# Gate products of an RG-LRU layer on Trainium2: two channel tiles in one group of 64-row matmuls, and a dummy square root ahead of the first x^T transfer

## The chip, the cores and the metric

The kernel runs on one core of one Trainium2 chip. A core has five engines, each with its own in-order instruction queue: TensorE (PE, with its weight loads shown apart as PEld), VectorE (DVE), ScalarE (ACT), GpSimd (POOL) and SyncE (SP, which here only issues transfers). They meet through semaphores. 16 DMA engines move data between the chip's memory (HBM) and the core's SBUF; TensorE writes into PSUM, which has eight banks of 128 x 512 float32. The metric is the device time of one execution in microseconds (us), as the median of several runs.

## The reference, cut to what matters

One layer: an FFN, then a mixer with two branches, then a second FFN, at sequence length 512 and model width 1024, in float32. The change touches the recurrent branch, on 1024 channels that form 16 blocks of 64:

```python
xr = causal_conv(xr, conv_w[l], conv_b[l])                    # 4 taps
xb = xf.reshape(b, s, LRU_BLOCKS, LRU_BLOCK)                  # 16 blocks of 64 channels
r  = sigmoid(einsum('bshi,hij->bshj', xb, wa) + ba)           # one 64x64 matrix per block
ig = sigmoid(einsum('bshi,hij->bshj', xb, wx) + bx)
log_a = -LRU_C * r * softplus(-lam)
a = exp(log_a)
u = sqrt(-expm1(2.0 * log_a)) * (ig * xf)
h[t] = a[t] * h[t-1] + u[t]                                   # scan over the sequence
y_a = (hr * gelu(xg)) @ w_lru_out[l]
```

At the very start, the first FFN multiplies the normalised input by `ffn1_w1` and `ffn1_w3`; the kernel works on x transposed (x^T), tile by tile of 128 channels.

## The kernel before, in words

**Precision.** Every float32 operand of a matmul is split into a high part (rounded, written by ScalarE) and a low part (the rest, written by VectorE), and each product is three matmuls: high by high, low by high, high by low. The function `split2` (from L189) does this for activations, `split_to` (from L149) for weights: L156 on ScalarE, L157 on VectorE.

**Units.** A projection of 128 output channels is a "unit": `unit` takes the next weight tile (`get`, which also splits the weights two units ahead and loads raw ones further ahead), takes a PSUM bank and runs 24 matmuls of 128 x 512 (`mm_feat`, L201 to L203). After every 12 of them it calls `point()`.

**The plan.** `later(n, fn, rank)` puts a piece of work n points ahead; `point()` counts one and runs what is due, by rank and then by the order in which it was put there. That sets where in each engine's queue the piece stands. There is no other scheduler: each engine then works through its queue in order.

**The stage of the change.** After the first FFN come units xr 0 to 7 (the recurrent input; xr 0 to 3 inside the function before), wg 0 to 7 (gates of the merge), wk 0 and 1, four products for v, wq 0 and 1, xg 0 to 7. Point 9 is the middle of unit wg0, point 13 that of wg2, point 17 that of wg4, point 21 that of wg6, point 25 that of wk0. Put among them by the tables at the file's end, for channel tile i (128 channels, two blocks of 64):

- `conv(i)` at `CONV_AT[i]`: L814 on ScalarE and three L816 on VectorE.
- `rg_gates(i)` at `RG_AT[i]` = 7, 11, 13, 15, 17, 19, 21, 23: splits the tile (L191 on ScalarE, L192 on VectorE, into `xcs`); two points later (`RG_LAG`) `products`: two banks, r and i, and six matmuls (L832) in three pairs. One of a pair uses rows 0 to 63 of the array, the other rows 64 to 127, each with a 64 x 128 weight that holds a block's two matrices side by side; one point later `gates`: four tanh of 64 x 512 on ScalarE (L837, L840), which empty the two banks, and L841 on VectorE.
- `rg_decay(i)` at `DECAY_AT[i]`: L852 and L853 on ScalarE, and one point later L856 to L858 on VectorE.
- `rg_scan(i)` at `SCAN_AT[i]`: a Sqrt on ScalarE (L866), later L869 and the scan L870 on VectorE.
- one point after each wg unit `gate_out` (L894 on ScalarE), which empties the unit's bank; after each wk unit `k_out` (L905 to L911), after each v product `v_out`, after each wq unit `q_out` (L943, L945), after each xg unit `y_out`, which needs the scan's result.

PSUM banks are handed out in turn, eight in all, so the ninth request waits until the first of the eight was read.

**The start.** Nine warm-up matmuls on zeros (L603); x^T tile 0 is loaded by a transfer that ScalarE issues (L591), then a Sqrt of a tiny tile (L609) loads the table that holds Sqrt; the other first transfers are issued by SP (`vec`, then the first weights and x^T tiles). Then, for each of eight x^T tiles, ScalarE writes the high part (L643), VectorE the low part (L644), and nine matmuls follow (L650 to L652). A hardware transfer signals one of eight semaphores in turn, so the ninth waits for the first.

Of the kernel before, what the change touches and what calls it, by code (L numbers as in the profile page):

```python
# [12 lines left out]
AF = mybir.ActivationFunctionType  # L13
ALU = mybir.AluOpType

P = 128
# [15 lines left out]
V_CW, V_CB, V_BA, V_BX, V_LAM, V_BG, V_G1, V_SINK, V_N = 0, 32, 40, 48, 56, 64, 80, 88, 104  # L32
# [19 lines left out]
def hybrid_layer(ctx: ExitStack, tc: tile.TileContext, a: dict, out: bass.AP):  # L52
    nc = tc.nc
    act, dve, pool, pe, sp = nc.scalar, nc.vector, nc.gpsimd, nc.tensor, nc.sync
# [8 lines left out]
    def slot(shape, dt=F32, name="s"):  # L63
        uid[0] += 1
        return sb.tile(shape, dt, tag="slot", name=f"{name}_{uid[0]}")

    def bank(name="ps"):
        uid[0] += 1
        return pp.tile([P, 512], F32, tag="ps", name=f"{name}_{uid[0]}")
# [14 lines left out]
    bxh = cp.tile([P, 2, KT], F32, name="bxh")  # L84
# [76 lines left out]
    def get(nm, i, ahead=2, rawahead=3):  # L161

        k = st["get"]
        assert order[k] == (nm, i), (order[k], nm, i)
        dma_to(k + 1 + ahead)
        split_to(k + 1 + ahead)
        dma_to(st["split"] + rawahead)
        st["get"] += 1
        return pairs.pop(k)
# [5 lines left out]
    def later(n, fn, rank=1):  # L175
        uid[0] += 1
        due.append((now[0] + n, rank, uid[0], fn))
# [11 lines left out]
    def split2(hi, lo, src):  # L189

        act.activation(hi, src, AF.Copy)  # L191
        dve.tensor_tensor(out=lo, in0=src, in1=f32(hi), op=ALU.subtract)  # L192
# [14 lines left out]
    def unit(nm, i, **kw):  # L207
        w = get(nm, i)
        ps = bank("f")
        mm_feat(ps, w, **kw)  # L210
        return ps
# [12 lines left out]
    def rstd_of(ssq, scale=1.0, during=lambda q: None):  # L224

        n = ssq.shape[-1]
        w = 1 if n == 2 else n
        v, q, r, e, r2 = (small(w, x) for x in ("v", "q", "r", "e", "r2"))
        if n == 2:
            dve.tensor_scalar(out=v, in0=ssq[:, 0:1], scalar1=ssq[:, 1:2], scalar2=D * EPS, op0=ALU.add, op1=ALU.add)  # L230
        else:
            dve.tensor_scalar(out=v, in0=ssq, scalar1=D * EPS, scalar2=None, op0=ALU.add)
        act.activation(q, v, AF.Sqrt)
        during(q)
        dve.reciprocal(r, q)
        if w == 1:
            dve.scalar_tensor_tensor(out=e, in0=r, scalar=v, in1=r, op0=ALU.mult, op1=ALU.mult)
        else:
            dve.tensor_tensor(out=e, in0=r, in1=r, op=ALU.mult)
            dve.tensor_tensor(out=e, in0=e, in1=v, op=ALU.mult)  # L240
        s = scale * D**0.5
        dve.tensor_scalar(out=e, in0=e, scalar1=-0.5 * s, scalar2=1.5 * s, op0=ALU.mult, op1=ALU.add)
        dve.tensor_tensor(out=r2, in0=r, in1=e, op=ALU.mult)
        return r2
# [345 lines left out]
    def load_x(k, q=sp):  # L590
        q.dma_start(out=xts[k // 2][:, k % 2, :], in_=a["xT"][k * P : (k + 1) * P, :])  # L591
# [10 lines left out]
    for _ in range(WARM):  # L602
        pe.matmul(psw, warm[:, :P], warm, start=True, stop=True)  # L603

    load_x(0, act)

    tiny = small(4, "tiny")
    dve.memset(tiny, 1.0)
    act.activation(tiny, tiny, AF.Sqrt)  # L609
    sp.dma_start(out=vec, in_=a["vec"])  # L610
    for kp in range(KT // 2):
        load_w(0, kp)
# [18 lines left out]
    ps = [bank("f") for _ in range(NS)]  # L631
# [28 lines left out]
    r = rstd_of(s4, during=lambda q: act.activation(tiny, q, AF.Silu))  # L660
# [129 lines left out]
    def rg_load():  # L790
        r = slot([P, KT, P], name="rgraw")
        for nm, cs in (("rg_a_w", (0, 64)), ("rg_x_w", (64, 0))):
            v = a[nm].rearrange("(i two) p q -> two p i q", two=2)
            for par, c in enumerate(cs):
                pool.dma_start(out=r[64 * par : 64 * par + 64, :, c : c + 64], in_=v[par])
        hi = slot([P, KT, P], F32R, name="rghi")
        lo = slot([P, KT, P], F32R, name="rglo")
        act.activation(hi, r, AF.Copy)
        dve.tensor_tensor(out=lo, in0=r, in1=f32(hi), op=ALU.subtract)
        return hi, lo  # L800

    rgw = rg_load()
# [4 lines left out]
    def hcol(base, i):  # L807
        return bhalf[:, base - V_BA + i : base - V_BA + i + 1]
# [11 lines left out]
    def rg_gates(i):  # L820
        s0 = lru[i]
        s1 = slot([P, 2, SEQ], name="ig_e")
        lru[i] = (s0, s1)
        xs = slot([P, 2, SEQ], F32R, name="xcs")
        xc, t, ig = s0[:, 0, :], s0[:, 1, :], s1[:, 0, :]
        split2(xs[:, 0, :], xs[:, 1, :], xc)

        def products():
            ps = bank("r"), bank("i")
            for n, (w, x) in enumerate(((0, 0), (1, 0), (0, 1))):  # L830
                for p_, r_ in zip(ps, (slice(0, 64), slice(64, P))):
                    pe.matmul(p_, rgw[w][r_, i, :], xs[r_, x, :], start=n == 0, stop=n == 2)  # L832

            def gates():
                lo_, up = slice(0, 64), slice(64, P)
                for p_, r_ in zip(ps, (lo_, up)):
                    act.activation(t[r_], p_[r_], AF.Tanh, scale=0.5, bias=hcol(V_BA, i)[r_])  # L837

                for par, (p_, r_, o_) in enumerate(((ps[0], up, lo_), (ps[1], lo_, up))):
                    act.activation(ig[o_], p_[r_], AF.Tanh, scale=0.5, bias=bxh[r_, par, i : i + 1])  # L840
                dve.scalar_tensor_tensor(out=ig, in0=ig, scalar=1.0, in1=xc, op0=ALU.add, op1=ALU.mult)  # L841

            later(1, gates, 2)

        later(RG_LAG, products)

    def rg_decay(i):
        s0, s1 = lru[i]  # L850
        t, ig, e = s0[:, 1, :], s1[:, 0, :], s1[:, 1, :]
        act.activation(e, t, AF.Exp, scale=cneg[:, i : i + 1], bias=cneg[:, i : i + 1])  # L852
        act.activation(t, t, AF.Tanh, scale=chalf[:, i : i + 1], bias=chalf[:, i : i + 1])  # L853

        def factors():
            dve.scalar_tensor_tensor(out=ig, in0=e, scalar=1.0, in1=ig, op0=ALU.add, op1=ALU.mult)  # L856
            dve.scalar_tensor_tensor(out=e, in0=e, scalar=1.0, in1=t, op0=ALU.add, op1=ALU.mult)
            dve.tensor_scalar(out=e, in0=e, scalar1=-1.0, scalar2=1.0, op0=ALU.mult, op1=ALU.add)  # L858

        later(1, factors, 3)  # L860

    def rg_scan(i):
        s0, s1 = lru[i]
        t, ig, a_ = s0[:, 1, :], s1[:, 0, :], s1[:, 1, :]

        act.activation(t, t, AF.Sqrt, scale=0.25)  # L866

        def scan():
            dve.tensor_tensor(out=ig, in0=t, in1=ig, op=ALU.mult)  # L869
            dve.tensor_tensor_scan(t, a_, ig, 0.0, op0=ALU.mult, op1=ALU.add)  # L870
            lru[i] = s0

        later(SCAN_LAG[i], scan, 3)
# [6 lines left out]
    for i, p in enumerate(RG_AT):  # L880
        later(p, lambda i=i: rg_gates(i))
    for i in range(8):
        later(DECAY_AT[i], lambda i=i: rg_decay(i), 3)
        later(SCAN_AT[i], lambda i=i: rg_scan(i), 3)
# [11 lines left out]
    for i in range(8):  # L896
        ps = unit("wg", i)
# [16 lines left out]
    for i in range(2):  # L914
        ps = unit("wk", i)
# [8 lines left out]
    for t in range(NT):  # L924
        ps = bank("v")
# [22 lines left out]
    for i in range(2):  # L948
        ps = unit("wq", i)
# [12 lines left out]
    for i in range(8):  # L962
        ps = unit("xg", i)
# [121 lines left out]
    for nm, i in att_units:  # L1085
        if nm == "lru":
            w = get(nm, i) if i else w_lru
            ps = bank("f")
# [5 lines left out]
        ps = unit(nm, i)  # L1094
# [4 lines left out]
    w = get("wao", 0)  # L1099
# [14 lines left out]
    for i in range(8):  # L1114
        if i:
            w = get("wao", i)
        ps = bank("f")
# [33 lines left out]
ATT_STEP = 2.2  # L1151
ATT_LAG = (1, 1, 4, 1, 3, 1)
RG_LAG = 2
DECAY_AT = (11, 15, 17, 19, 21, 23, 25, 27)
SCAN_AT = (29, 29, 30, 30, 31, 31, 32, 32)
SCAN_LAG = (1, 2, 2, 3, 3, 4, 4, 5)
NSLOT = 42
# [59 lines left out]
```

## Time and profile before

| | us |
|---|---|
| median of 3 runs (1138.6 to 1138.85) | 1138.76 |
| profiled execution | 1138.66 |
| its span | 1136.9 |
| TensorE busy | 1128.2 |
| VectorE busy | 778.7 |
| ScalarE busy | 582.2 |

The granted TensorE clock was 0.998 over the span. The profile lists, for one execution, how long each engine was busy, the span in 40 equal slices (each digit the busy share in tenths), the chain of work that ended last, followed back from the end, groups of equal instructions, waits with what ended them, and instructions in order of time. A row of the last view has the start in us from the span's start, the duration, the engine, the line of the kernel, the operation, the output and the inputs by the program's names, the shape and a count; in square brackets stands the idle time of the engine just before and what ended it. Matmuls overlap in the array: what counts there is the distance from start to start, not the duration.

### The profile page before, as it was taken

How to read it: one execution, taken by the hardware profiler on the slowest of the kernel's cores; microseconds unless marked ns; L12 is line 12 of the kernel's file. 1: busy time of each engine (PE TensorE's matmuls, PEld its weight loads, DVE VectorE, ACT ScalarE, POOL GpSimd, SP SyncE). 2: the span in 40 equal slices, each digit the busy share in tenths (PEclk: the TensorE clock that was granted, in tenths of full speed). 3: DMA queues.
4: the chain of work that ended last, by engine and by line, in shares of the span. 5: the costliest groups of instructions: out<-in, count | busy, mean ns of one | idle time of the engine just before them, and what ended most of it. 6: DMA issues, size and time to landing. Idle time of an engine off the chain costs nothing.

```text
span 1136.9 us, 17091 instructions
## 1 busy us (share of the span) xinstructions
PE 1128.2 (99%) x6691; PEld 1001.0 (88%) x6691; DVE 778.7 (68%) x1183; ACT 582.2 (51%) x1036; POOL 340.7 (30%) x257
## 2 busy tenths in 40 slices
PE   9999999999999999999999999999999999999997
PEld 7889999988889977888888888889899999998886
DVE  5997889885436745684778854667968678985313
ACT  7445555564325369944656652356445555574211
POOL 0148677500001000001555640000655567700000
PEclk9999999999999999999999999999999999999999
DMA  9943223264314311334122333532123332254101
GB/s 343 158 132 112 96 92 111 82 216 157 104 55 146 132 56 56 90 96 130 56 85 83 93 109 98 176 118 93 39 93 112 112 103 84 93 193 176 40 19 55
DMA packets 36800, 124.93 MB, mean 110 GB/s; under 512 B 4400, under 2 KB 5936, under 8 KB 36720
## 3 DMA queue, kind: packets, MB, share of 16 engines
q1 hardware_dynamic: 34128, 115.15, 30.3%
q0 software_dynamic: 2448, 8.43, 3.8%
q8 instruction: 52, 0.85, 0.3%
q10 hardware_dynamic: 144, 0.26, 0.1%
q14 instruction: 28, 0.23, 0.1%
HBM read 116.50 MB, written 7.33 MB: 109 GB/s over the span
## 4 chain that ended last, share of the span: by engine, by line
PE 97%; DVE 2%; ACT 0%; issue 0%; DVEq 0%
PE f L201 11%; PE f L202 11%; PE f L203 11%; PE c L454 10%; PE c L453 10%; PE c L452 10%; PE acc L220 8%; PE acc L221 8%; PE acc L219 8%; PE pt L1032 1%; PE s L996 1%; PE s L995 1%; PE tr L292 1%; PE r L832 1%; PE o L1048 1%; PE o L1049 1%
## 5 line engine op out<-in xcount | busy, mean ns | idle before, releaser
L201 PE MATMUL f<-uT,whi 128*128 128x512 f32 (+1 forms) x536 | 197.1, 368 | 0.0
L202 PE MATMUL f<-uT,wlo 128*128 128x512 f32 (+1 forms) x536 | 195.3, 364 | 0.3 <-DVE wlo L157 0.3
L203 PE MATMUL f<-uT,whi 128*128 128x512 f32 (+1 forms) x536 | 195.0, 364 | 0.0
L219 PE MATMUL acc<-whi,hT 128*128 128x512 f32 x352 | 137.1, 390 | 0.0
L220 PE MATMUL acc<-wlo,hT 128*128 128x512 f32 x352 | 137.0, 389 | 0.0
L221 PE MATMUL acc<-whi,hT 128*128 128x512 f32 x352 | 136.9, 389 | 0.0
L201 PEld LDWEIGHTS f<-uT,whi 128*128 128x128 f32 x536 | 101.1, 189 | 18.4 <-issue 2.9
L192 DVE TENSOR_TENSOR wlo<-S,whi 128x1024 fp32r<-128x1024 f32 x68 | 112.9, 1660 | 4.0 <-ACT whi L191 3.7
L453 PE MATMUL c<-Xh,wlo 128*128 128x256 f32 x408 | 115.5, 283 | 0.0
L454 PE MATMUL c<-Xl,whi 128*128 128x256 f32 x408 | 115.5, 283 | 0.0
L453 PE MATMUL c<-uT,wlo 128*128 128x256 f32 x408 | 115.5, 283 | 0.0
L454 PE MATMUL c<-uT,whi 128*128 128x256 f32 x408 | 115.5, 283 | 0.0
L452 PE MATMUL c<-Xh,whi 128*128 128x256 f32 x408 | 115.5, 283 | 0.0
L452 PE MATMUL c<-uT,whi 128*128 128x256 f32 x408 | 115.5, 283 | 0.0
L202 PEld LDWEIGHTS f<-uT,wlo 128*128 128x128 f32 x536 | 101.2, 189 | 16.1 <-DVE wlo L157 0.7
L203 PEld LDWEIGHTS f<-uT,whi 128*128 128x128 f32 x536 | 101.1, 189 | 16.1
L1016 POOL TENSOR_SCALAR P<-P,d 128x256 f32<-128x256 f32 (+1 forms) x64 | 63.8, 1011 | 55.5 <-DVE d L1014 33.2
L452 PEld LDWEIGHTS c<-Xh,whi 128*128 128x128 f32 x408 | 78.3, 192 | 0.0
L452 PEld LDWEIGHTS c<-uT,whi 128*128 128x128 f32 x408 | 78.3, 192 | 0.0
L453 PEld LDWEIGHTS c<-uT,wlo 128*128 128x128 f32 x408 | 78.3, 192 | 0.0
L453 PEld LDWEIGHTS c<-Xh,wlo 128*128 128x128 f32 x408 | 78.3, 192 | 0.0
L454 PEld LDWEIGHTS c<-Xl,whi 128*128 128x128 f32 x408 | 78.3, 192 | 0.0
(309 smaller groups left out, 2684.5 us busy)
## 6 DMA issues: line engine op xcount, KB each, us to landing
raw_w2a<-in_w2a_dram SPq DMA_DIRECT2D x22, 512.0 KB, 3.7
raw_w1b<-in_w1b_dram SPq DMA_DIRECT2D x22, 512.0 KB, 4.0
raw_w3b<-in_w3b_dram SPq DMA_DIRECT2D x22, 512.0 KB, 3.9
raw_w2b<-in_w2b_dram SPq DMA_DIRECT2D x22, 512.0 KB, 4.2
raw_w3a<-in_w3a_dram SPq DMA_DIRECT2D x21, 512.0 KB, 4.4
raw_w1a<-in_w1a_dram SPq DMA_DIRECT2D x20, 512.0 KB, 4.4
raw_wg<-in_wg_dram SPq DMA_DIRECT2D x16, 512.0 KB, 3.8
raw_xr<-in_xr_dram SPq DMA_DIRECT2D x8, 512.0 KB, 4.1
```

Of the source, the lines that this page charges most:

```text
L192: dve.tensor_tensor(out=lo, in0=src, in1=f32(hi), op=ALU.subtract)
L201: pe.matmul(ps[:, c0:c1], wh[:, s], h_, start=k == 0, stop=False)
L202: pe.matmul(ps[:, c0:c1], wl[:, s], h_, start=False, stop=False)
L203: pe.matmul(ps[:, c0:c1], wh[:, s], l_, start=False, stop=k == KT - 1)
L219: pe.matmul(acc[n], x[:, 0, c], wh[:, s], start=first, stop=False)
L220: pe.matmul(acc[n], x[:, 0, c], wl[:, s], start=False, stop=False)
L221: pe.matmul(acc[n], x[:, 1, c], wh[:, s], start=False, stop=last)
L292: pe.transpose(ps[:, k * P : (k + 1) * P], hg[:, kk * P : (kk + 1) * P], ident)
L452: pe.matmul(ps, wh[:, s], xh, start=first, stop=False, skip_group_check=True)
L453: pe.matmul(ps, wl[:, s], xh, start=False, stop=False, skip_group_check=True)
L454: pe.matmul(ps, wh[:, s], xl, start=False, stop=k == 3, skip_group_check=True)
L1016: pool.tensor_scalar(out=pt[:, x, b0:256], in0=pt[:, x, b0:256], scalar1=d[:, x : x + 1], scalar2=None, op0=ALU.mult)
```

## The change

The gate products are gathered in a list, `rg_wait`. `rg_gates(i)` appends tile i; for odd i it puts `products` two points ahead, and `products` takes two banks for every tile in the list, then runs all their matmuls behind one another, puts `gates` of each one point ahead, and empties the list. `gates` is the same work as before. `DECAY_AT` has other points. At the start the load of x^T tile 0 is moved behind the tiny Sqrt on ScalarE's queue.

```diff
-    load_x(0, act)
 
     tiny = small(4, "tiny")
     dve.memset(tiny, 1.0)
     act.activation(tiny, tiny, AF.Sqrt)
+    load_x(0, act)
     sp.dma_start(out=vec, in_=a["vec"])
...
         def products():
-            ps = bank("r"), bank("i")
-            for n, (w, x) in enumerate(((0, 0), (1, 0), (0, 1))):
-                for p_, r_ in zip(ps, (slice(0, 64), slice(64, P))):
-                    pe.matmul(p_, rgw[w][r_, i, :], xs[r_, x, :], start=n == 0, stop=n == 2)
-
-            def gates():
...
-            later(1, gates, 2)
-
-        later(RG_LAG, products)
+
+            for p in rg_wait:
+                p["ps"] = bank("r"), bank("i")
+            for p in rg_wait:
+                for n, (w, x) in enumerate(((0, 0), (1, 0), (0, 1))):
+                    for p_, r_ in zip(p["ps"], (slice(0, 64), slice(64, P))):
+                        pe.matmul(p_, rgw[w][r_, p["i"], :], p["xs"][r_, x, :], start=n == 0, stop=n == 2)
+                later(1, p["gates"], 2)
+            rg_wait.clear()
+
+        def gates():
+            lo_, up = slice(0, 64), slice(64, P)
+            ps = me["ps"]
...
+        me = {"i": i, "xs": xs, "gates": gates}
+        rg_wait.append(me)
+        if i % 2:
+            later(RG_LAG, products)
+
+    rg_wait = []
...
-DECAY_AT = (11, 15, 17, 19, 21, 23, 25, 27)
+DECAY_AT = (15, 16, 19, 20, 23, 24, 27, 28)
```

More of the change, by code (lines that the diff above doesn't have):

```diff
@@ L828, in products @@
         def products():
-            ps = bank("r"), bank("i")
-            for n, (w, x) in enumerate(((0, 0), (1, 0), (0, 1))):
-                for p_, r_ in zip(ps, (slice(0, 64), slice(64, P))):
-                    pe.matmul(p_, rgw[w][r_, i, :], xs[r_, x, :], start=n == 0, stop=n == 2)
-            def gates():
[L835 to L841, printed above, removed]
-            later(1, gates, 2)
-        later(RG_LAG, products)
+            for p in rg_wait:
[9 more added lines that the diff above has]
+            ps = me["ps"]
+            for p_, r_ in zip(ps, (lo_, up)):
+                act.activation(t[r_], p_[r_], AF.Tanh, scale=0.5, bias=hcol(V_BA, i)[r_])
+            for par, (p_, r_, o_) in enumerate(((ps[0], up, lo_), (ps[1], lo_, up))):
+                act.activation(ig[o_], p_[r_], AF.Tanh, scale=0.5, bias=bxh[r_, par, i : i + 1])
+            dve.scalar_tensor_tensor(out=ig, in0=ig, scalar=1.0, in1=xc, op0=ALU.add, op1=ALU.mult)
+        me = {"i": i, "xs": xs, "gates": gates}
[3 more added lines that the diff above has]
+    rg_wait = []
     def rg_decay(i):
```

## The prediction

> **What bounds the kernel now.** I read the page first: span, busy shares, the chain that ended last, then the waits.
>
> ```profile
> span 1136.9 us, 17091 instructions
> PE 1128.2 (99%) x6691; PEld 1001.0 (88%) x6691; DVE 778.7 (68%) x1183; ACT 582.2 (51%) x1036; POOL 340.7 (30%) x257
> ACT  7445555564325369944656652356445555574211
> PE 97%; DVE 2%; ACT 0%; issue 0%; DVEq 0%
> PE f L202 <- DVE wlo L157: 0.3, 1, 0.3
> ```
>
> TensorE is busy 99% and is 97% of the chain; the longest wait of a matmul on another engine that the table of waits names after the start is 0.3 us. So time is won only by TensorE work or mode changes that go away, and any wait that the change puts in front of a matmul is added one for one. ScalarE is half busy as a mean, but the two nines in its row (slices of 28.4 us, so 426 to 483 us) are the stage that the change rearranges. There the mean says nothing: ScalarE's queue must be walked.
>
> The view of instructions in time shows what one group of gate products costs TensorE, and when it runs:
>
> ```profile
> 418.20 0.49 PE L832 MATMUL r<-xcs,rghi 64*128 64x512 f32 x1
> ...
> 420.36 0.39 PE L203 MATMUL f<-uT,whi 128*128 128x512 f32 x1
> ...
> 424.44 0.39 PE L203 MATMUL f<-uT,whi 128*128 128x512 f32 x1
> 424.75 0.49 PE L832 MATMUL r<-xcs,rghi 64*128 64x512 f32 x1
> ...
> 425.09 0.39 PE L832 MATMUL r<-xcs,rglo 64*128 64x512 f32 x1
> ...
> 425.65 0.50 PE L201 MATMUL f<-uT,whi 128*128 128x512 f32 x1
> 425.99 0.40 PE L202 MATMUL f<-uT,wlo 128*128 128x512 f32 x1
> ...
> 427.14 0.39 PE L201 MATMUL f<-uT,whi 128*128 128x512 f32 x1
> ```
>
> From 420.36 to 424.44 are 18 full matmuls: 0.227 us each, so 2.72 us for half a unit (12, one "point" of the plan). From 424.44 to 427.14 are 7 such steps (1.59) and one group: the group costs 2.70 - 1.59 = 1.11 us. Its three pairs (two 64-row matmuls start together) take 0.68 at full pace; the other 0.43 is the change of mode, there and back.
>
> **What the change removes.** The program's order shows what the diff does not: the groups are of three, two, two and one tiles, not of two. `rg_gates(2)` stands at point 13, as `products` of tiles 0 and 1 does, and was queued earlier, so tile 2 is already in `rg_wait`; the same happens with tiles 4 (point 17) and 6 (point 21). Eight groups become four with the same 48 matmuls: 4 x 0.43 = 1.7 us less on TensorE. Bounds: 0 (if the changes cost as much per tile) to 1.7.
>
> **What it adds.** The lag of two points between a tile's split and its products (5.44 us) was the cover for the split. For tiles 2, 4 and 6 it is now zero, and the 4 tanh of each tile come in bursts of 12, 8, 8 and 4 on ScalarE, ahead of other things in its in-order queue. The queue's prices:
>
> ```profile
> 412.92 0.82 ACT L853 ACTIVATE xc_t<-xc_t,chalf 128x512 f32<-128x512 f32 x1
> 413.64 1.04 ACT L156 ACTIVATE whi<-raw_wg 128x1024 fp32r<-128x1024 f32 x1
> ...
> 419.20 0.69 ACT L837 ACTIVATE xc_t<-r,bhalf 64x512 f32<-64x512 f32 x1 [2.92 <-PE r L832]
> ...
> 422.03 1.06 ACT L156 ACTIVATE whi<-raw_wg 128x1024 fp32r<-128x1024 f32 x1
> 423.00 0.61 ACT L191 ACTIVATE xcs<-xc_t 128x512 fp32r<-128x512 f32 x1
> 423.51 0.67 ACT L894 ACTIVATE g<-f,bhalf 128x512 f32<-128x512 f32 x1
> 424.09 0.80 ACT L852 ACTIVATE ig_e<-xc_t,cneg 128x512 f32<-128x512 f32 x1
> 424.92 0.82 ACT L853 ACTIVATE xc_t<-xc_t,chalf 128x512 f32<-128x512 f32 x1
> 425.76 0.68 ACT L837 ACTIVATE xc_t<-r,bhalf 64x512 f32<-64x512 f32 x1
> ```
>
> Start to start: a tile's 4 tanh 2.83; a weight split (L156) 0.97; a tile's split (L191) 0.51, done after 0.61; a `gate_out` (L894) 0.58, done after 0.67; one decay 0.83 + 0.72 = 1.55 when a copy follows (412.92 to 413.64). VectorE's half of a tile's split comes behind that of a weight:
>
> ```profile
> 411.12 1.23 DVE L157 TENSOR_TENSOR wlo<-raw_wg,whi 128x1024 fp32r<-128x1024 f32 x1 [0.40 <-ACT whi L156]
> 412.26 0.68 DVE L192 TENSOR_TENSOR xcs<-xc_t,xcs 128x512 fp32r<-128x512 f32 x1
> ...
> 415.97 0.68 DVE L192 TENSOR_TENSOR xcs<-xc_t,xcs 128x512 fp32r<-128x512 f32 x1
> ```
>
> The low half is ready 0.06 + 1.14 + 0.68 = 1.88 us after the L156 before it ends.
>
> I now walk the new order on the old clock. *Group 1* (tiles 0, 1, 2) stands where tile 1's group stood (418.20), one group earlier: 417.09. Tile 2 is split in time: its low half was there at 416.65 even before, and tile 0's tanh and decay no longer stand ahead of it. The tanh start 1.00 us after the first pair (418.20 to 419.20): 418.09. Twelve take 8.49, to 426.58; then a weight split, tile 3's split and, at 428.06, `gate_out(2)`, done 428.73. It empties the bank of unit wg2. Eight banks go round, and six are now taken by one group, so unit wg4 takes wg2's: TensorE gets there at 417.09 + 0.43 + 9 x 0.227 + 36 x 0.227 = 427.73 and waits to 428.79. **Stall one: 1.06 us**, a bank's release, not the tile.
>
> *Group 2* (tiles 3, 4): half a unit later TensorE is at 431.5. ScalarE leaves `gate_out(2)` at 428.64, then come two decays (3.10), a weight split (to 432.71, done 432.80), and tile 4's split, done 433.32; its low half at 434.68. Tile 3's pairs and the mode change bring TensorE to 432.5 (with 0.1 for the restart after stall one), and its last pair would run at 432.95; it runs at 434.74. **Stall two: 1.8 us.**
>
> *Group 3* (tiles 5, 6): `gate_out(3)` follows at 433.22, leaves 433.80; 8 tanh (5.66), weight split, tile 5's split, `gate_out(4)`, two decays bring the next weight split to 444.62, done 445.68, and tile 6's low half to 447.56. TensorE leaves group 2 at about 435.1, does four half units (10.9), enters the group (0.2), does five pairs (1.13) and wants it at 447.35. **Stall three: 0.2 us.** *Group 4* (tile 7) keeps its lag of two points: nothing.
>
> Each wait also costs a restart; the start of the program shows it (matmul at 8.71 after a wait, next 0.33 later, not 0.227):
>
> ```profile
> 8.27 0.40 PE L651 MATMUL f<-uT,wlo 128*128 128x512 f32 x1
> 8.71 0.50 PE L652 MATMUL f<-uT,whi 128*128 128x512 f32 x1
> 9.04 0.39 PE L650 MATMUL f<-uT,whi 128*128 128x512 f32 x1
> ```
>
> Most of these vanish in the next stall, whose end ScalarE sets; about 0.2 stays. Sum of the waits: 1.06 + 1.8 + 0.2 + 0.2 = 3.3 us. Bounds: 2.0 (if the queue runs a tenth faster than these rows) to 4.5 (a tenth slower, and a weight split late once).
>
> `DECAY_AT` puts the decays at least one point behind their gates again; its cost is in the walk, since nothing on TensorE waits for a decay before the scans. The next place with little cover is the weights of the xg units:
>
> ```profile
> 484.83 1.20 DVE L157 TENSOR_TENSOR wlo<-raw_xg,whi 128x1024 fp32r<-128x1024 f32 x1
> ...
> 489.34 1.20 ACT L943 ACTIVATE QS<-f 64x512 fp32r<-64x512 f32 x2 [3.29 <-PE f L203]
> ```
>
> The first low half was ready at 486.03, TensorE free for it at about 489: 3 us of cover. The debt left on ScalarE is about 2 us and TensorE is itself 1.6 later: hidden. Without that cover each us more would be a us.
>
> **The dummy root.** What moves is one Sqrt with its table load, now ahead of x^T tile 0's transfer on ScalarE's queue.
>
> ```profile
> 0.73 0.40 ACTq L591 DMA_DIRECT2D xt<-in_xT_dram  x1
> ...
> 1.17 1.28 ACT L609 ACT_TABLE_LOAD   x1 [1.17 <-PEq L1205]
> ...
> 2.46 0.21 ACT L609 ACTIVATE tiny<-tiny 128x4 f32<-128x4 f32 x1
> ...
> 4.00 0.43 SPq L596 DMA_DIRECT2D raw_first<-in_w3a_dram  x1
> ...
> 4.33 0.71 ACT L643 ACTIVATE uT<-xt,vec 128x512 fp32r<-128x512 f32 x1
> xt<-in_xT_dram ACTq DMA_DIRECT2D x1, 256.0 KB, 2.9
> vec<-in_vec_dram SPq DMA_DIRECT2D x1, 52.0 KB, 2.6
> ```
>
> The table load starts at 0.73, the root at 2.02, so the transfer is issued between 2.02 and 2.23 instead of 0.73 (earliest 1.41, when the root's operand is set, if the sequencer runs ahead). With 2.6 to 2.9 to land it is there at 4.0 to 5.1; I take 4.85. The first scaled tile started at 4.33, so the first matmul moves 0.5 later. Then two waits already there take it back: the twelfth matmul stood at 8.71 behind a low half of x^T tile 1, which SP fetches; it came 0.44 after the eleventh and 0.33 ahead of the next, against 0.227 each, so 0.3 us of the delay disappear in a wait that is there anyway. SP's transfer of 4.00 (w3a) waits for x^T tile 0's semaphore, eight transfers back, so SP's queue behind it slips to about 4.9. The view by stages shows what covers that: from 5 to 10 us the DMA engines are full (share 1.02), so transfers stand in line already, and one issued later only joins the line later.
>
> ```profile
> 5.00:10.00 5.00, 4.96 (x19) 3.37 (x18) 3.62 (x8) 3.60 (x9) 0.00 (x0) 1.00 1.02 342
> ```
>
> So I take 0.2 us lost, from -0.3 (weights land sooner with x^T out of their way) to 0.8 (nothing absorbed).
>
> **Sum**, against the profiled execution's 1138.66 us (span 1136.9; it lies 0.1 below the runs' median): 1138.66 - 1.7 + 3.3 + 0.2 = 1140.5 us (1140.46).
>
> **The rivals.**
>
> *A, not slower:* the queue of ScalarE doesn't reach TensorE. For it: ScalarE idled 2.92 us before the gates at 419.20, and TensorE as a whole waited for nothing there. Against it: that idle time lies ahead of group 1, the burst behind it. Time 1138.66 - 1.7 + 0.2 = 1137.2.
>
> *B, the start in full:* the slip of SP's queue is not covered, and 0.8 is paid in place of 0.2: 1141.1. For it: ScalarE and TensorE both work from hand to mouth until 9 us. Against it: 1.02 of DMA share from 5 to 10 us means transfers wait already.
>
> *C, the debt travels on:* the scans and the xg weights come late by more than 3 us, at 486 to 500 us, because VectorE also carries the bursts. A stall of 1 to 2 us more: 1142. Decided by the first wait at an xg unit's low half.
>
> *D, a colder clock:* the rows of the first 5 us hold 9 matmuls that took 4.21 us, 0.47 each, double the 0.227. If a stall brought that pace back for some 15 matmuls, 15 x 0.24 = 3.6 us: 1144.1. Against it: the longest unbroken wait in my walk is about 1 us.
>
> ```profile
> 1.45 4.21 PE L603 MATMUL w<-warm 128*128 128x512 f32 x9 [1.45 <-DVE tiny L608]
> ```
>
> [...]
>
> **How the numbers follow.** Forecast 0.57 (its own range 1139.3 to 1141.7), A 0.15, B 0.11, C 0.12, D 0.05. A measurement tells 0.2% from no change, 2.3 us: slower than 1141.04 or faster than 1136.5. The forecast lies within with 0.44 of its 0.57, A with 0.10, B with half of its 0.11: together 0.60 within 0.2%. The upper part of the forecast (0.13), the other half of B, C and D make slower 0.35; faster is the third of A in which the groups gain more than I count: 0.05. The range 1138.0 to 1142.2 leaves out D, most of A and the far end of C.
>
> **What would show it.** Right: four groups at TensorE of 9, 6, 6 and 3 pairs; idle time before wg4's first matmul with `gate_out` as releaser; a wait inside group 2 for `xcs` of ScalarE, then VectorE; ScalarE without a gap from about 418 to 440; x^T tile 0's transfer issued at about 2.1. Wrong: groups without idle time in them, TensorE past group 4 earlier than before (A), a wait at the first xg unit (C), 0.4 us steps behind a stall (D), or a first 10 us that end 0.5 us or more later (B).

## The result, and the profile after

| | before | after |
|---|---|---|
| median, us (6 runs each, same chip) | 1138.8 (1138.6 to 1138.87) | 1142.59 (1141.37 to 1143.12) |
| ratio, 95% interval | | 1.0032 [1.0019, 1.0045] |
| profiled execution, us | 1138.66 | 1142.08 |
| its span, us | 1136.9 | 1140.3 |
| mean granted clock | 0.998 | 0.995 |

The changed kernel is slower by 0.3%. It was forecast at 1140.5, the range ended at 1142.2, and the median lies 0.4 us outside it. The runs of the changed kernel also spread over 1.75 us where those of before spread over 0.3; that is part of the answer.

In the changed kernel the gate products stand at L835 (L832 before), the tanh at L843 and L846, the decays at L861 and L862 (ScalarE) and L865 to L867 (VectorE), `gate_out` at L903. From its page, the busy times and the row of the granted clock:

```profile
PE 1129.6 (99%) x6691; PEld 1003.5 (88%) x6691; DVE 778.5 (68%) x1183; ACT 581.3 (51%) x1036; POOL 341.3 (30%) x257
PEclk9999999999999998999999999999999999999999
```

The number of matmuls is the same, 6691, yet TensorE is busy 1.4 us longer. The last row points to the reason: one slice of 40, from 427.6 to 456.1 us, has a granted clock below nine tenths. In the row of before every slice reads 9:

```profile
PEclk9999999999999999999999999999999999999999
```

The waits of TensorE's matmuls from 410 to 510 us have one line, and it names the split of a channel tile (behind the colon: us in total, how often, the longest in us):

```profile
PE r L835 <- ACT xcs L191: 1.9, 1, 1.9
```

The instructions of TensorE in order of time show group 2 (tiles 3 and 4), and what follows it:

```profile
430.07 0.49 PE L835 MATMUL r<-xcs,rghi 64*128 64x512 f32 x1
...
430.64 0.39 PE L835 MATMUL r<-xcs,rghi 64*128 64x512 f32 x1
...
432.90 0.79 PE L835 MATMUL r<-xcs,rghi 64*128 64x512 f32 x1 [1.86 <-ACT xcs L191]
...
433.49 0.62 PE L835 MATMUL r<-xcs,rglo 64*128 64x512 f32 x1
...
434.24 0.79 PE L835 MATMUL r<-xcs,rghi 64*128 64x512 f32 x1
...
434.96 0.79 PE L201 MATMUL f<-uT,whi 128*128 128x512 f32 x1
435.55 0.63 PE L202 MATMUL f<-uT,wlo 128*128 128x512 f32 x1
435.98 0.63 PE L203 MATMUL f<-uT,whi 128*128 128x512 f32 x1
...
439.39 0.53 PE L202 MATMUL f<-uT,wlo 128*128 128x512 f32 x1
439.76 0.39 PE L203 MATMUL f<-uT,whi 128*128 128x512 f32 x1
```

Tile 3's three pairs run at 430.07 to 430.64. Tile 4's first pair would be due at 430.87 and runs at 432.90, after an unbroken pause of 1.86 us. From there each matmul comes 0.43 after the last (435.55, 435.98 and on) instead of 0.227, until 439.39. The view by stretches of time gives the clock itself (columns after the window: length, then busy time and count of PE, PEld, DVE, ACT, POOL; then granted clock, DMA share, GB/s):

```profile
420.00:430.00 10.00, 10.00 (x45) 8.05 (x43) 4.71 (x7) 9.82 (x15) 0.00 (x0) 1.00 0.18 52
430.00:433.00 3.00, 1.14 (x9) 0.59 (x8) 1.62 (x3) 2.97 (x5) 0.00 (x0) 0.98 0.01 3
433.00:436.40 3.40, 3.28 (x9) 1.84 (x10) 3.20 (x6) 3.34 (x6) 0.00 (x0) 0.50 0.45 151
436.40:439.80 3.40, 3.40 (x10) 2.68 (x9) 1.10 (x2) 3.34 (x5) 0.00 (x0) 0.52 0.03 8
439.80:443.00 3.20, 3.20 (x16) 2.63 (x15) 2.86 (x4) 3.17 (x6) 0.00 (x0) 1.00 0.29 42
```

The full clock was granted until the pause, half of it for 6.8 us behind the pause, and the full clock again after that.

*Where the time went.* Two landmarks: the first matmul of L668, at the end of the start, and the first full matmul (128 rows) behind the last group, that of tile 7. From TensorE's instructions in order of time, of before:

```profile
28.20 0.81 PE L668 MATMUL e<-oh 32*16 32x384 f32 x2
...
458.44 0.50 PE L201 MATMUL f<-uT,whi 128*128 128x512 f32 x1
```

and of after:

```profile
27.74 0.81 PE L668 MATMUL e<-oh 32*16 32x384 f32 x2
...
461.85 0.50 PE L201 MATMUL f<-uT,whi 128*128 128x512 f32 x1
```

The stage ends 3.41 us later. In these two executions 0.46 was gained at the start, and 1.7 is due from four mode changes fewer (1.70 measured with `pairs_scan_noroot`, below), so group 2 and what follows it cost 5.6 us. The experiments divide that into waits and clock.

### The profile page after: what moved, and what is told of

Same layout as the page of the kernel before. It is cut to its first block, busy times and chain, and to the rows that moved or that the text cites. A ratio compares the mean times of both kernels' runs of the same rounds, so it can differ in the third digit from the quotient of the medians.

```text
span 1140.3 us, 17100 instructions
## 1 busy us (share of the span) xinstructions
PE 1129.6 (99%) x6691; PEld 1003.5 (88%) x6691; DVE 778.5 (68%) x1183; ACT 581.3 (51%) x1036; POOL 341.3 (30%) x257
## 4 chain that ended last, share of the span: by engine, by line
PE 93%; DMA 2%; DVE 2%; ACT 2%; issue 0%; SPq 0%; DVEq 0%
PE f L201 11%; PE f L202 11%; PE f L203 11%; PE c L454 10%; PE c L453 10%; PE c L452 10%; PE acc L219 8%; PE acc L220 8%; PE acc L221 8%; DMA raw_w3a<-in_w3a_dram 2%; PE pt L1041 1%; PE s L1005 1%; DMA xt<-in_xT_dram 1%; PE s L1004 1%; PE tr L292 1%; PE o L1057 1%
## 5 line engine op out<-in xcount | busy, mean ns | idle before, releaser
L452 PEld LDWEIGHTS c<-uT,whi 128*128 128x128 f32 x408 | 78.3, 192 | 0.0
L454 PEld LDWEIGHTS c<-uT,whi 128*128 128x128 f32 x408 | 78.3, 192 | 0.0
```

Of the source, the lines that this page charges most:

```text
L452: pe.matmul(ps, wh[:, s], xh, start=first, stop=False, skip_group_check=True)
L454: pe.matmul(ps, wh[:, s], xl, start=False, stop=k == 3, skip_group_check=True)
```

## The experiments

Each was timed together with the kernel before, whose median was 1138.47 to 1138.59 us there. Diffs are against the changed kernel unless said otherwise.

### The two parts apart

`root_only` is the kernel before with the dummy root moved ahead of the transfer, and nothing else; `group_only` is the changed kernel with the transfer put back ahead:

```diff
+    load_x(0, act)
     tiny = small(4, "tiny")
     dve.memset(tiny, 1.0)
     act.activation(tiny, tiny, AF.Sqrt)
-    load_x(0, act)
```

> Only the move of x^T tile 0's transfer behind the tiny Sqrt; gate products as before. Theory (the start gains: the third weight tile lands 0.5 us sooner and the two waits of the first twelve matmuls go): 0.4 to 0.5 us below before, 1138.3, with the matmul that stood at 28.20 at about 27.74. Rival (the start is neutral and the 0.46 us in the changed kernel is chance): within 0.1 us of before.

Measured: 1138.45 us (11 runs, 1138.12 to 1138.94), ratio 1.0 [0.9991, 1.0009]. ScalarE's instructions at the start of `root_only`:

```profile
0.73 1.28 ACT L608 ACT_TABLE_LOAD   x1 [0.73 <-PEq L1205]
1.46 0.38 ACTq L591 DMA_DIRECT2D xt<-in_xT_dram  x1
2.02 0.21 ACT L608 ACTIVATE tiny<-tiny 128x4 f32<-128x4 f32 x1
...
4.44 0.72 ACT L643 ACTIVATE uT<-xt,vec 128x512 fp32r<-128x512 f32 x1 [0.50 <-DMA xt<-in_xT_dram]
```

The transfer is issued at 1.46, while the table load (0.73 to 2.01) still runs and before the root ahead of it in the queue has started. The order in the queue held the transfer back by 0.73 us, not by the 1.3 to 1.5 that a wait for the table would cost, and the first scaled tile started 0.11 later than before (4.44 against 4.33). The time is that of before, as the rival had it; the gain of 0.4 to 0.5 us did not come.

> Only the grouped gate products and the new DECAY_AT; the start as before. Theory (one wait of some 2 us in group 2, then half clock for about 6.8 us): 0.46 us above the changed kernel, about 1143.0, runs spread by more than 1 us. Rival (the start's shift causes the coincidence that makes the wait): no half clock, about 1139.5.

Measured: 1141.43 us (6 runs: 1139.91, 1139.99, 1141.38, 1141.49, 1142.52, 1143.12), ratio 1.0026 [1.0014, 1.0037]. Its profiled execution (span 1140.7) has the same pause of 1.86 us and the same steps of 0.43 behind it. So the loss sits in the grouping. The time is not 0.46 above the changed kernel, as expected, but 1.2 below it: putting the transfer back cost nothing that shows. Two of the six runs are 1.4 us below the next: the same program, some executions of which lose less.

### Fill the pause: is it the wait or the clock?

`fill8` and `fill4` put eight or four extra pairs of 64-row matmuls in front of tile 4's own. Their sums are overwritten by tile 4's first product, so this is TensorE work without use, in time that is idle anyway.

```diff
-            for p in rg_wait:
+            for q, p in enumerate(rg_wait):
+                if p["i"] == 4:
+                    o = rg_wait[q - 1]
+                    for _ in range(8):
+                        for p_, r_ in zip(p["ps"], (slice(0, 64), slice(64, P))):
+                            pe.matmul(p_, rgw[0][r_, o["i"], :], o["xs"][r_, 0, :], start=True, stop=True)
```

> The changed kernel with 8 extra pairs of 64-row matmuls ahead of tile 4's own in group 2 (1.8 us of work at 0.227 a pair); they go into tile 4's banks and are overwritten by its own products. Theory A (TensorE's idle time of 1.9 us in group 2 makes the clock drop): no step of 0.43 us behind group 2, granted clock 1.00 there, time 1138.7 - 0.5 - 1.7 + 2.6 = 1139.1, spread of the runs small again. Rival B (the slow steps come from ScalarE and VectorE reading banks or SBUF during the burst): steps of 0.43 stay, 1142 or more. Rival C (the pause is not idle time but the whole loss is the wait for tile 4): no change, 1142.6.

Measured: 1139.86 us (11 runs, 1139.65 to 1140.32), ratio 1.0012 [1.0003, 1.002]. More matmuls, and 2.7 us less than the changed kernel. Group 2 of `fill8`, in order of time (the products stand at L840 here, the extra ones at L837):

```profile
432.45 0.39 PE L837 MATMUL r<-xcs,rghi 64*128 64x512 f32 x1
...
432.86 0.50 PE L840 MATMUL r<-xcs,rghi 64*128 64x512 f32 x1
...
434.20 0.49 PE L840 MATMUL r<-xcs,rghi 64*128 64x512 f32 x1 [0.61 <-DVE xcs L192]
...
434.62 0.50 PE L201 MATMUL f<-uT,whi 128*128 128x512 f32 x1
434.96 0.40 PE L202 MATMUL f<-uT,wlo 128*128 128x512 f32 x1
435.20 0.40 PE L203 MATMUL f<-uT,whi 128*128 128x512 f32 x1
...
437.29 0.39 PE L203 MATMUL f<-uT,whi 128*128 128x512 f32 x1
```

Tile 4 runs at the same time as in the changed kernel (432.86 against 432.90, the low half at 434.20 against 434.24): the split, not TensorE, sets it. But no step of 0.43 follows. From the first pair (430.03) to the next full matmul (434.62) are 4.59 us; two tiles that don't wait need 1.59 (experiment `pairs`, 429.31 to 430.90). So the waits cost 3.0 us, and the half clock 1142.59 - 1139.86 = 2.7 (2.5 when each median is taken against that of before which was measured with it). The two traces show the same by themselves: from tile 4's last pair to the twelfth full matmul behind it are 5.52 us in the changed kernel (434.24 to 439.76) and 3.09 in `fill8` (434.20 to 437.29), 2.43 more for the same matmuls. Theory A held for the clock. Its time, 1139.1, was too low because it took 0.5 us off for the start and counted 2.6 for the waits.

> As the kernel with 8 extra pairs, with 4: about 1.0 us of TensorE's idle time ahead of tile 4's pairs is left in place of 1.9, then the wait for the low half (0.6 to 0.8). The end of the wait is set by ScalarE and VectorE, so without a clock drop the time is that of 8 pairs, 1139.9. Theory (the drop needs about 2 us of idle time): 1139.9 with a small spread. Rival (any idle time near 1 us can do it, by chance of phase): some executions at 1141 to 1143, median above 1140.5.

Measured: 1140.19 us, ratio 1.0016 [1.0007, 1.0025]: eight of eleven runs at 1140.02 to 1140.5, three at 1141.13 to 1141.31. The profiled execution, one of the eight, pauses twice and keeps its pace:

```profile
433.38 0.49 PE L840 MATMUL r<-xcs,rghi 64*128 64x512 f32 x1 [0.94 <-ACT xcs L191]
...
434.72 0.50 PE L840 MATMUL r<-xcs,rghi 64*128 64x512 f32 x1 [0.61 <-DVE xcs L192]
435.15 0.50 PE L201 MATMUL f<-uT,whi 128*128 128x512 f32 x1
435.49 0.40 PE L202 MATMUL f<-uT,wlo 128*128 128x512 f32 x1
```

The three slower runs were not profiled; that the clock made them slower is read from their mean clock (0.997 to 0.998, against 0.998 to 0.999), no more.

### Give the tiles their lag back

`pairs` runs the products ahead of a split that is due at the same point. `rg_gates(2)` then comes too late for group 1, so the groups are tiles 0-1, 2-3, 4-5 and 6-7, and each odd tile has its full lag of two points.

```diff
-            later(RG_LAG, products)
+            later(RG_LAG, products, 0)
```

> The changed kernel with products run ahead of rg_gates of the same point (rank 0), so that the groups are tiles 0-1, 2-3, 4-5, 6-7, each with the full lag of two points behind its last split. Theory (the loss is the wait for a tile split in the same point): no wait in the groups, no half clock, 1138.7 - 0.5 - 1.7 = 1136.5. Rival (bursts of 8 tanh alone hold up ScalarE's splits): a wait of 0.5 us or more in a group or at a unit's weights, 1137 or more, above 1139 if the clock drops.

Measured: 1137.26 us (11 runs, 1137.13 to 1137.7), ratio 0.999 [0.9981, 0.9999]. Group 2 and the full matmul behind group 4:

```profile
429.31 0.49 PE L835 MATMUL r<-xcs,rghi 64*128 64x512 f32 x1
...
430.90 0.50 PE L201 MATMUL f<-uT,whi 128*128 128x512 f32 x1
...
456.28 0.50 PE L201 MATMUL f<-uT,whi 128*128 128x512 f32 x1
```

Six pairs without a pause, and 456.28 against 458.44 of before: 2.16 less, of which 0.45 is the start (L668 at 27.75) and 1.71 the modes. Then part is given back. The waits of TensorE's weight loads from 480 to 510 us name the low half of the xg weights, written by VectorE; in the changed kernel the same view is empty:

```profile
PEld f L202 <- DVE wlo L157: 0.9, 2, 0.5
```

TensorE is early now, and VectorE has two scans ahead of the first of these weights: two steps of TensorE, 486.99 to 487.44 and 498.23 to 498.61 (the first and the third xg unit), stand where 0.227 belongs, about 0.4 us too long together, 0.6 with the longer step behind each. `pairs_scan` moves the scans of tiles 2 to 7 one point later, `pairs_scan_noroot` has the transfer ahead of the root as well:

```diff
-SCAN_LAG = (1, 2, 2, 3, 3, 4, 4, 5)
+SCAN_LAG = (1, 2, 3, 4, 4, 5, 5, 6)
```

> The kernel with groups 0-1, 2-3, 4-5, 6-7, and in addition SCAN_LAG (1, 2, 3, 4, 4, 5, 5, 6): the scans of tiles 2 to 7 one point later, so that VectorE writes the low halves of the xg weights 1.9 us sooner. Theory (the last 0.6 us that the pairs lost are the two waits at xg units, 0.45 and 0.38 steps and their restarts): no wait there, 1137.26 - 0.6 = 1136.7. Rival (the later scans hold up y_out instead): same as with pairs or slower, with waits at the xg or lru units.

> The same with the load of x^T tile 0 back ahead of the tiny Sqrt. Theory (the move of the root is worth nothing that can be told: the first twelve matmuls run at either pace by chance of the clock's warm-up): within 0.3 us of pairs_scan. Rival (the move gains the 0.46 us seen in the changed kernel's profile): 0.4 to 0.5 us slower than pairs_scan.

Measured: `pairs_scan` 1136.61 us (11 runs, 1136.35 to 1137.13), ratio 0.9983 [0.9974, 0.9992]; `pairs_scan_noroot` 1136.85 (1136.57 to 1137.3), ratio 0.9984 [0.9976, 0.9993]. Without the root and without waits the grouping gives 1138.55 - 1136.85 = 1.70 us, the four mode changes. The root's 0.24 on top isn't told apart from nothing. `pairs_scan` beats both kernels.

### Two ways to have the split earlier

`decay_late` takes the two decays out of ScalarE's queue ahead of tile 4's split, and moves the later ones likewise:

```diff
-DECAY_AT = (15, 16, 19, 20, 23, 24, 27, 28)
+DECAY_AT = (17, 17, 21, 21, 25, 25, 27, 28)
```

> The changed kernel with only DECAY_AT moved to (17, 17, 21, 21, 25, 25, 27, 28): the groups stay of three, two, two and one tiles and tile 4 is still split in the point of its own products, but the decays of tiles 0 to 3 now stand behind the splits of tiles 4 and 6 on ScalarE (3.1 us each time). Theory (the wait is ScalarE's queue: burst, two decays, weight split, then tile 4's split): tile 4's high half is ready at about 429.7 and its low half at 431.1, TensorE wants them at 430.9 and 431.3, so no wait over 0.3 us and no half clock; 1137.0 to 1137.5, and the weights of the xg units may add up to 0.6 as in the kernel with pairs. Rival (zero lag alone is enough to make the wait, whatever stands ahead): a wait over 1 us in group 2 and 1140 or more.

Measured: 1141.38 us, ratio 1.0021 [1.0012, 1.003]; five runs at 1139.8 to 1140.22, six at 1141.38 to 1142.6. Group 2 lost its wait (430.72 to 432.31 in one go), as the theory said, but the time hardly moved: the wait is now in group 3. TensorE's instructions of `decay_late` in order of time:

```profile
445.61 0.50 PE L835 MATMUL r<-xcs,rghi 64*128 64x512 f32 x1 [1.46 <-DVE xcs L192]
...
447.34 0.49 PE L835 MATMUL r<-xcs,rghi 64*128 64x512 f32 x1 [0.77 <-DVE xcs L192]
...
447.77 0.66 PE L201 MATMUL f<-uT,whi 128*128 128x512 f32 x1
448.23 0.63 PE L202 MATMUL f<-uT,wlo 128*128 128x512 f32 x1
```

and VectorE's ahead of them:

```profile
436.75 0.69 DVE L847 SCALAR_TENSOR_TENSOR ig_e<-ig_e,xc_t 128x512 f32<-128x512 f32 x1 [5.04 <-ACT ig_e L846]
439.55 0.69 DVE L847 SCALAR_TENSOR_TENSOR ig_e<-ig_e,xc_t 128x512 f32<-128x512 f32 x1 [2.10 <-ACT ig_e L846]
440.16 0.68 DVE L865 SCALAR_TENSOR_TENSOR ig_e<-ig_e 128x512 f32<-128x512 f32 x1
...
443.73 1.22 DVE L157 TENSOR_TENSOR wlo<-raw_wg,whi 128x1024 fp32r<-128x1024 f32 x1
444.87 0.68 DVE L192 TENSOR_TENSOR xcs<-xc_t,xcs 128x512 fp32r<-128x512 f32 x1
```

VectorE idles 5.04 and 2.10 us behind ScalarE's tanh, and then has both tiles' decay factors (440.16 to 443.7) in front of the weight and the low half that TensorE waits for. A second queue, in order as well, took the debt over.

`lag1` leaves the groups at 3, 2, 2 and 1 tiles, and splits tiles 2, 4 and 6 one point earlier:

```diff
-RG_AT = (7, 11, 13, 15, 17, 19, 21, 23)
+RG_AT = (7, 11, 12, 15, 16, 19, 20, 23)
```

> The groups stay 3, 2, 2 and 1 tiles, but tiles 2, 4 and 6 are split one point (2.72 us) earlier (RG_AT 12, 16 and 20 in place of 13, 17 and 21), and so also ahead of one decay and of one weight split in ScalarE's queue. Theory (the wait comes from the split's place in the queue, not from the size of the burst): the high part of tile 4 is ready at about 430.3 to 431, its low part at about 431.7, and TensorE wants them at 430.9 and 431.3, so the wait in group 2 is at most 0.5 us, no step of 0.43 follows it, and the time is 1137.3 to 1137.9 (up to 0.6 us of it at the xg units, as with four groups of two). Rival (twelve tanh in a row hold ScalarE up wherever the split stands): a wait of more than 1 us in group 2, the half clock behind it in at least some runs, and 1139.5 or more.

Measured: 1137.22 us (11 runs, 1137.04 to 1137.62), ratio 0.9989 [0.998, 0.9998]. ScalarE of `lag1` still has the twelve tanh in a row, up to 426.3; tile 4's split stands one decay and one weight split further ahead:

```profile
428.39 0.81 ACT L861 ACTIVATE ig_e<-xc_t,cneg 128x512 f32<-128x512 f32 x1
...
429.94 0.61 ACT L191 ACTIVATE xcs<-xc_t 128x512 fp32r<-128x512 f32 x1
...
432.02 1.04 ACT L156 ACTIVATE whi<-raw_wg 128x1024 fp32r<-128x1024 f32 x1
```

The high half is there at 430.55, and VectorE's low half (430.59, 0.69 us) at 431.28; TensorE takes them at 431.10 and 431.56 without a pause. So the burst of twelve tanh alone costs nothing in group 2. What cost 3.0 us was the split's place behind two decays and a weight split with no lag left. At the xg units two steps of TensorE in `lag1` (487.54 to 487.84 and 498.29 to 498.67) are too long, 0.3 us with the longer step behind the second; `lag1` with the later scans was not tried.

## Why the prediction was wrong, point by point

**Mode changes: right.** 1.70 us, seen at the landmark of `pairs` and as the whole gain of `pairs_scan_noroot`. Groups of 3, 2, 2 and 1 tiles ran as read from the program's order.

**Stall one: wrong, 1.06 us that did not come.** The text on the kernel says that banks are handed out in turn. They are not: unit wg4's first matmul ran at 427.26, and `gate_out(2)`, which empties wg2's bank, only at 427.59, so wg4 had another bank and did not have to wait. By the author's reading of the program it was tile 0's r bank, last read by the tanh from 419.09 to 419.78; the trace does not name banks, so that is not shown. TensorE's row of the changed kernel:

```profile
427.26 0.39 PE L201 MATMUL f<-uT,whi 128*128 128x512 f32 x1
```

and ScalarE's in the same stage:

```profile
427.59 0.68 ACT L903 ACTIVATE g<-f,bhalf 128x512 f32<-128x512 f32 x1
...
431.29 1.04 ACT L156 ACTIVATE whi<-raw_wg 128x1024 fp32r<-128x1024 f32 x1
432.23 0.61 ACT L191 ACTIVATE xcs<-xc_t 128x512 fp32r<-128x512 f32 x1
```

**Stall two: its end was right, its length not.** The walk put tile 4's high part at 433.32 and its low part at 434.68 on the old clock, 432.86 and 434.22 with the start 0.46 earlier. These ScalarE rows give 432.23 + 0.61 = 432.84, and VectorE's low half was done at 434.18:

```profile
433.50 0.68 DVE L192 TENSOR_TENSOR xcs<-xc_t,xcs 128x512 fp32r<-128x512 f32 x1
```

With stall one gone TensorE came there 1.1 us sooner and spent the whole debt in one place. Together the waits cost 3.0 us, where the sum had 3.3 for stalls one to three and the restarts. That the two are close is no luck: ScalarE's queue sets the end of stall two, so what TensorE doesn't wait for at wg4 it waits for in group 2. Stall three, 0.2, did not show: TensorE came later, with nothing left to wait for.

**The step that failed: rival D, put at 0.05.** "Against it: the longest unbroken wait in my walk is about 1 us." The mechanism, the sign by which it would show (0.4 us steps behind a stall) and roughly its size (15 steps at 0.24, 3.6 us; measured 2.4 to 2.7) stood there, but the sum has no term for the clock, and the range leaves D out. What spoke against D was the length of a wait, and that hung on how banks are handed out. With the debt in one pause of 1.86 us the clock fell, and the median paid 2.7 us that the sum put at nothing. On the walk's own waits 0.05 was low as well: `fill4`, with pauses of 0.94 and 0.61, has three slower executions in eleven. Without the clock the forecast would have stood: 1138.66 - 1.7 + 3.0 = 1139.96, and `fill8`, which pays the waits alone, measured 1139.86, inside the forecast's own range.

No row of before shows how long a pause must be to bring such steps, so that 1 us is too short for it was the author's estimate. The runs showed a granted clock of 0.50 from 433.0 on, behind one pause of 1.86 us. What makes one execution slower and another with the same pauses not, no run shows.

**The dummy root: 0.2 lost was foreseen, nothing measured.** The transfer went out at 1.46, near the early bound (1.41) and not at 2.02 to 2.23, the value taken. The start does vary: L668 ran at 27.74 in the changed kernel, 28.20 before, and 28.38 in `root_only`, whose median is that of before. So 0.4 us of a single profile's start says nothing of the root. The starts differ in pace: the first matmuls of L650 to L652 stand 0.43 apart until 7.59 in `root_only`, and only one step is longer than 0.33 in the changed kernel (5.45 to 5.98). The granted clock of the changed kernel reads 1.00 from 5 to 10 us, the long step included; for `root_only` the record has the mean over its span, 0.999. So the reason stays open, and that the clock sets the pace there, as the expectation of `pairs_scan_noroot` has it, is not shown.

**Rivals A, B and C.** A's condition, a queue that doesn't reach TensorE, isn't met by this change, but by `lag1` and `pairs` in the groups. That both measure A's 1137.2 is in part luck: A adds 0.2 for the root, which no run shows, and has nothing for the xg units; without waits there the grouping reaches 1136.6 to 1136.9. B did not occur. C's place, the first xg unit, is where `pairs` begins to lose its 0.6 us and `lag1` its 0.3. The changed kernel doesn't wait there, as foreseen, because TensorE is late itself.

## What to carry to other kernels

Work that is grouped to save mode changes is worth 0.43 us a group here, and that is less than one late operand (3.0 us of waits in group 2): before grouping, list which items are in the queue when the group runs, in the program's own order, and how long each one's operand was finished before. A pause of TensorE had two prices here, the wait (3.0 us) and the clock behind it (2.4 to 2.7 us); put both into the range as soon as a single pause may come near 1 us (0.94 in `fill4`, where three of eleven executions were slower), and find out which of the two was paid by filling the pause with matmuls whose results are not used. Here it helped to split the late tile earlier (`lag1`) or to leave it to the next group (`pairs`); thinning the queue in front of its split (`decay_late`) moved the debt to the next engine.

## What the runs showed of the hardware

Whether the half clock follows a pause differs between executions of one kernel, and by the times it followed more often the longer the idle time was. The times of `group_only`, `decay_late` and `fill4` fall into a lower cluster and runs at least 0.6 us above it; the table counts the latter, and gives how far they lie above the lower cluster's median. The changed kernel has no run in a lower cluster and so is set against that of `group_only`, which has the same products and the same pause:

| kernel | pauses in group 2 (or 3), us | executions above | how far, us |
|---|---|---|---|
| after | 1.86, then about 0.3 | 6 of 6 | 1.4 to 3.2 |
| group_only | 1.86, then 0.48 | 4 of 6 | 1.4 to 3.2 |
| decay_late | 1.46, 0.77 | 6 of 11 | 1.4 to 2.6 |
| fill4 | 0.94, 0.61 | 3 of 11 | 1.0 to 1.2 |
| fill8 | 0.61 | 0 of 11 | none |

The half clock lasted 6.8 us in the profiled execution of the changed kernel, and about 3.4 us in that of `decay_late` (granted clock 0.62 over 447.5 to 452.0, as 3.4 of the 4.5 us at half would give; steps of 0.42 to 0.46 from 447.77 to 451.21, of 0.23 from 451.52 on). No sharp threshold shows: with 0.94 us of idle time and 0.61 behind it some executions were slower and others not. Only profiled executions show the clock by stretches, so for the rest of the table the cause is read from the times and the mean clock, and is not shown one by one. The two agree: of the ten slower executions of the changed kernel and `group_only`, those 1.4 to 1.5 us above have a mean clock of 0.997 or 0.998, those 2.1 to 3.2 above have 0.995.

ScalarE's queue issues a transfer while a table load ahead of it still runs: in `root_only` 1.46 us against a load from 0.73 to 2.01 and an activation at 2.02. The root ahead of the transfer moved it from 0.73 to 1.46, not behind the load. What set 1.46 was not tested.
